# Sending the last unit of a seven-product SwiGLU by halves of tokens, and a job that runs its own last products

## The chip, the cores and the metric

One core of one Trainium2 chip. The metric is the device time of one launch in microseconds (us); lower is better. The engines are named as in the profile: PE is TensorE (PEld its weight loads), DVE is VectorE, ACT is ScalarE, POOL is GpSimd, SP is SyncE. SPq is the queue on which SP issues DMAs, POOLq that of POOL.

## The reference, cut to what matters

The kernel is one step of a hybrid streaming encoder over 1072 tokens (16 meta tokens, 1024 new frames, 32 frames of a running stream). Two feed-forward nets (FFN1 at the start, FFN2 at the end) stand around a mixing layer of attention and a recurrent branch. The change touches only the two nets:

```
def half_ffn(x, g, w_gate, w_up, w_down):
    h = rmsnorm(x, g)
    return x + 0.5 * ((jax.nn.silu(h @ w_gate) * (h @ w_up)) @ w_down)
```

The model width is 1024 and the hidden width of the nets is 2816. All operands are float32 and every product is made as three float32r products (high x high, high x low, low x high), so each operand is kept as a "hi" and a "lo" part.

## The kernel before, in words

Both nets run through the class `Seven`. It computes matrix products in a Strassen-like form, with seven block products in place of eight. The names of the operands on the token side are B11, T3, B21, T2, T4, T1, B22. The hidden width is cut into 22 chunks of 128 and these into 11 pairs, called **units** 0 to 10. The tokens are cut into four quarters of `qw` columns (268 in FFN1, 264 in FFN2): a half `b` (0 or 1) of the tokens and, in it, a token block `th`.

**The gate and up products** (`rest`, `unit`). For each unit two passes are made, gate and up, each of seven steps (`first` to `seventh`), each step for b = 0 and b = 1. A step is 12 matmuls for one b. Steps one, three and four copy their bank out on ACT; the others are added and multiplied on DVE. Only in the up pass of the last unit are all seven steps of b = 0 made ahead of those of b = 1, because then the operands of b = 0 (tiles xh0 and xl0) come free early and the next stage can load into them.

**Sending** (`send`). When a unit's result g is complete, its seven operands for the down products are formed: for four of them a subtraction on DVE (L359), for each a hi copy on ACT (L219) and a lo subtraction on DVE (L220) into a place, and then one DMA on POOL's queue (L371) into `mid_dram`. Each send covers both halves b: 128 x 2 x 264 or 268 columns, hi and lo, 536 or 528 KB. The places are `R` (one buffer) and `st` (one buffer), by turns. The works wait in the list `later`, and `tick` takes one of them after every second step (after every step in the gate pass of the last unit). The last unit's seven works are all sent from within `down`, four ahead of its first products and three behind them. They use the places of the list `stages`: R, e, e, st, s, s, R. Here "e" are two tiles that operands of the last unit leave free, and "s" two tiles of partial sums of that unit. Unit 2 is later loaded into the two "e" places and into `st`.

**The down products** (`down`). A **job** accumulates two units into two chunks of the output. It has seven products p1 to p7; p1 fills a bank `pv`, which ACT copies to a bank `pu` (L618), and p4 adds to `pu`. The results go out on ACT (first time, L612) or DVE (L609). The first four jobs take unit 0 alone, for one b at a time (3 matmuls a product, banks ps_z and ps_o). The jobs of the main run take two units and both b (12 matmuls a product). In `run` the order of the products of one job is p1, p6 of the job before, p2, p3, p7 of the job before, p4, p5: the last two products of a job are run within the next job. A job marked "end" has its p4 ahead of its p3, its p6 ahead of its p5, and its p7 at the very end. While jobs run, the order of PE's instructions is fixed by hand (`PE.on`). Elsewhere, and on the other engines throughout, the framework's scheduler puts the instructions of an engine into an order at build time by its own estimate of when each can start, the earlier in the program first; on the chip each engine runs that order.

**Loading** (`Home`, `home`). The operands of a unit are read back from `mid_dram` on SP's queue: one transfer for each b, and one or two more for the operands that do not fit. Units use three sets of places by turns (unit number modulo 3). Unit s+1 is loaded when the jobs of step s begin, into the places of unit s-2. In the main run steps s = 1 to 10 have two jobs each, (0, 1) or (2, 3); step 9 has only job 0 and step 10 only job 2. Thus unit 10 is loaded into the places of unit 7, which the second job of step 8 is the last to read, and job 2 of step 10 reads it first.

`lanes` reads and splits the weights of a job (raw, g, whi, wlo), on SP's queue, ACT and DVE.

Of the kernel before, what the change touches and what calls it, by code (L numbers as in the profile page):

```python
# [9 lines left out]
F32 = mybir.dt.float32  # L10
F32R = mybir.dt.float32r
BF16 = mybir.dt.bfloat16
AF = mybir.ActivationFunctionType
ALU = mybir.AluOpType
AX = mybir.AxisListType

P = 128
# [14 lines left out]
NAMES = ("B11", "T3", "B21", "T2", "T4", "T1", "B22")  # L32
D_FF = 2816
FC = D_FF // P
# [48 lines left out]
def tile_encoder_step(ctx, tc, x_prompt, x_sample, cache_k, cache_v, state_hgrn, meta_tokens,  # L83
# [4 lines left out]
    nc = tc.nc  # L88
# [129 lines left out]
    def split(dst_h, dst_l, src):  # L218
        A.activation(dst_h, src, AF.Copy)  # L219
        V.tensor_tensor(dst_l, src, dst_h.bitcast(F32), op=ALU.subtract)  # L220
# [108 lines left out]
    class Seven:  # L329
# [6 lines left out]
        def __init__(self, pool, t0, qw, w_gate, w_up, mids, tags, homes):  # L336
            self.pool, self.t0, self.qw, self.w_gate, self.w_up, self.tags = pool, t0, qw, w_gate, w_up, tags
            self.mids, self.homes = mids, homes
            self.B, self.X, self.ahead = {}, {}, {}
            self.gs, self.later, self.groups = [], [], 0  # L340
            self.stages = ["R", "e", "e", "st", "s", "s", "R"]

        def tile(self, name, shape, dt=F32):
            tag, bufs = self.tags[name]
# [6 lines left out]
        def send(self, i, gs):  # L351

            def part(c, th):
                return gs[c][:, self.t0:].rearrange("p (b t n) -> p b t n", b=2, t=2)[:, :, th]

            def away(name, v, left=None, right=None):
                def work():
                    if left is not None:
                        V.tensor_tensor(v, left, right, op=ALU.subtract)  # L359
                    at = self.stages.pop(0) if i == FC // 2 - 1 else ("R", "st")[len(self.later) % 2]  # L360
                    shape = [P, 2, 2, self.qw]
                    if at == "R":
                        st = base.tile(shape, F32R, tag="R", name="st")
                    elif at == "st":
                        st = self.pool.tile(shape, F32R, tag="st", name="st", bufs=1)
                    elif at == "e":
                        st = self.early.pop(0)
                    else:
                        st = self.tile(at, shape, F32R)
                    split(st[:, :, 0], st[:, :, 1], v)  # L370
                    nc.gpsimd.dma_start(self.mids[i, :, :, NAMES.index(name)], st.bitcast(F32))  # L371
                self.later.append(work)
            b11, b12, b21, b22 = (part(c, th) for c in range(2) for th in range(2))
            away("B11", b11)
            away("T1", b11, b12, b11)
            away("B21", b21)
            away("T3", b12, b22, b12)
            away("B22", b22)
            away("T2", b22, b22, b11)
            away("T4", b21, b21, b22)  # L380

        def tick(self, every=2):
            self.groups += 1
# [38 lines left out]
        def unit(self, w, i, gs, gate):  # L422

            qw, where, hilo, X = self.qw, self.where, self.hilo, self.X
            raws = []
            for x in range(2):
                raw = self.tile("raw2", [P, D]) if x else wp.tile([P, D], F32, tag="raw", name="raw", bufs=2)
                c = 2 * i + x
                nc.sync.dma_start(raw.rearrange("p (k m) -> p k m", k=KC),
                                  w[0][:, c * P:(c + 1) * P].rearrange("(k p) m -> p k m", p=P))  # L430
                raws.append(raw)
            a11, a12, a21, a22 = (r[:, x:x + 512] for r in raws for x in (0, 512))
            A11, A12 = hilo(raws[0], D)
            sa = self.tile("S", [P, D])
            s2, s1 = sa[:, :512], sa[:, 512:]
            V.tensor_tensor(s1, a21, a22, op=ALU.add)
            V.tensor_tensor(s2, s1, a11, op=ALU.subtract)
            S2, S1 = hilo(sa, D)
            sb = self.tile("S", [P, D])
            V.tensor_tensor(sb[:, :512], a11, a21, op=ALU.subtract)  # L440
            V.tensor_tensor(sb[:, 512:], a12, s2, op=ALU.subtract)
            S3, S4 = hilo(sb, D)
            A22, = hilo(a22, 512)

            def out(c, th, b, part, ps):
                to = where(gs[c], th, b)
                if gate:
                    if part is not None:
                        V.tensor_tensor(to, part, ps[:, :qw], op=ALU.add)
                    silu(to, ps[:, :qw] if part is None else to)  # L450
                else:
                    if part is not None:
                        V.tensor_tensor(part, part, ps[:, :qw], op=ALU.add)
                    V.tensor_tensor(to, ps[:, :qw] if part is None else part, to, op=ALU.mult)

            parts = [self.tile("s", [P, 4, qw]) for b in range(2)]
            x, y, z = {}, {}, {}

            def first(b):
                x[b] = bank(rotate=True)  # L460
                product(x[b], A11, X["B11", b], True)
                A.activation(parts[b][:, 0], x[b][:, :qw], AF.Copy)

            def second(b):
                z[b] = bank(rotate=True)
                product(z[b], A12, X["B21", b], True)
                out(0, 0, b, parts[b][:, 0], z[b])

            def third(b):
                product(x[b], S2, X["T2", b], False)  # L470
                A.activation(parts[b][:, 1], x[b][:, :qw], AF.Copy)

            def fourth(b):
                y[b] = bank(rotate=True)
                product(y[b], S1, X["T1", b], True)
                A.activation(parts[b][:, 2], y[b][:, :qw], AF.Copy)

            def fifth(b):
                product(x[b], S3, X["T3", b], False)
                out(1, 1, b, parts[b][:, 2], x[b])  # L480

            def sixth(b):
                product(y[b], S4, X["B22", b], False)
                out(0, 1, b, parts[b][:, 1], y[b])

            def seventh(b):
                product(x[b], A22, X["T4", b], False)
                out(1, 0, b, None, x[b])

            steps = first, second, third, fourth, fifth, sixth, seventh  # L490
            if i == FC // 2 - 1 and not gate:
                for b in range(2):
                    for step in steps:
                        step(b)
            else:
                for step in steps:
                    for b in range(2):
                        step(b)
                    self.tick(1 if i == FC // 2 - 1 else 2)

        def rest(self):
            for i in range(1, FC // 2):
                gs = [self.tile("g", [P, T]) for _ in range(2)]
                self.unit(self.w_gate, i, gs, True)
                self.unit(self.w_up, i, gs, False)
                while self.later:
                    self.later.pop(0)()
                self.send(i, gs)

        class Home:  # L510

# [62 lines left out]
        def down(self, w, resid, final, after, early):  # L574
# [70 lines left out]
            def run(jobs):  # L645

                queue, count, every = [], [0], [1]

                def step(product):
                    product()  # L650
                    count[0] += 1
                    if queue and count[0] % every[0] == 0:
                        queue.pop(0)()
                before = None
                for job in jobs:
                    step(job.p1)
                    if before:
                        step(before.p6)
                    step(job.p2)
                    step(job.p4 if job.done == "end" else job.p3)  # L660
                    if before:
                        step(before.p7)
                        if before.done:
                            queue += before.done()
                            every[0] = max(1, 20 // len(queue))
                    step(job.p3 if job.done == "end" else job.p4)
                    if job.done == "end":
                        step(job.p6)
                    step(job.p5)
                    before = job  # L670
                if before.done != "end":
                    before.p6()
                before.p7()
                while queue:
                    queue.pop(0)()

# [29 lines left out]
            def steps():  # L706
                for s in range(1, last + 1):
                    for mp in ((0, 1) if s % 2 else (2, 3)):
# [8 lines left out]
                        job = Job([(units[s - 1], W, 0), (units[s], W, 1)], mp)  # L717
                        if s == last and mp == 2:
                            job.done = "end"
                        yield job  # L720

            psum("pairs")
# [1133 lines left out]
```

## Time and profile before

| | |
|---|---|
| three runs | 2469.76, 2469.8 and 2472.51 us, median 2469.8 |
| the profiled execution | 2468.0 us, of which the span of its instructions is 2466.2 |
| busy in the span | PE 97%, PEld 93%, DVE 68%, ACT 41%, POOL 10% |
| granted TensorE clock | 0.994 of full speed over the span |
| FFN1's last up pass, b = 1, and its first down jobs | about 503 to 531 us of the span |
| end of FFN1's main run of jobs | about 683 to 722 |
| the same two places in FFN2 | about 2200 to 2226 and 2378 to 2414 |

The page's first part gives busy time by engine. The timeline lists instructions with their start and length; a bracket behind a row gives how long the engine stood idle before it and what ended that idle time. The view of windows gives busy time by stretch, with the granted clock (PEclk) and the share of the core's 16 DMA engines. The view of the DMA queues splits traffic between q1 (transfers issued by SP) and q0 (those issued by POOL), and gives for each issue the time from issue to landing.

### The profile page before, as it was taken

How to read it: one execution, taken by the hardware profiler on the slowest of the kernel's cores; microseconds unless marked ns; L12 is line 12 of the kernel's file. 1: busy time of each engine (PE TensorE's matmuls, PEld its weight loads, DVE VectorE, ACT ScalarE, POOL GpSimd, SP SyncE). 2: the span in 40 equal slices, each digit the busy share in tenths (PEclk: the TensorE clock that was granted, in tenths of full speed). 3: DMA queues.
4: the chain of work that ended last, by engine and by line, in shares of the span. 5: the costliest groups of instructions: out<-in, count | busy, mean ns of one | idle time of the engine just before them, and what ended most of it. 6: DMA issues, size and time to landing. Idle time of an engine off the chain costs nothing.

```text
span 2466.2 us, 47916 instructions
## 1 busy us (share of the span) xinstructions
PE 2396.0 (97%) x19500; PEld 2292.9 (93%) x19500; DVE 1669.0 (68%) x3144; ACT 1017.8 (41%) x2129; POOL 257.1 (10%) x461
## 2 busy tenths in 40 slices
PE   6999999999999999999999999999799999999997
PEld 5999999989999998899888888999799999999997
DVE  4866676767766477764666665556966767676876
ACT  6444444442225233332445544323444444453223
POOL 1011010100003012121000000112011111110000
PEclk9999999999999999999999999999899999999999
DMA  7334343487652111111211122522234444468761
GB/s 199 106 127 164 124 168 123 160 315 280 244 211 79 50 44 48 57 48 50 59 45 45 49 67 62 193 87 100 75 130 150 140 150 141 152 239 323 272 237 72
DMA packets 270371, 331.93 MB, mean 135 GB/s; under 512 B 41078, under 2 KB 228726, under 8 KB 264518
## 3 DMA queue, kind: packets, MB, share of 16 engines
q1 hardware_dynamic: 247942, 244.96, 29.7%
q0 software_dynamic: 22208, 83.91, 9.0%
q8 instruction: 153, 2.51, 0.4%
q14 instruction: 68, 0.56, 0.1%
HBM read 213.93 MB, written 114.89 MB: 133 GB/s over the span
## 4 chain that ended last, share of the span: by engine, by line
PE 84%; DVE 5%; issue 5%; DMA 4%; ACT 2%; POOL 1%; SPq 0%; DVEq 0%; ACTq 0%; POOLq 0%
PE ps_mm L103 28%; PE ps_z L103 26%; PE ps_o L103 9%; PE pu L103 6%; PE ps_tr L103 5%; PE pf L103 4%; PE pv L103 4%; PE ps_tr L106 2%; DMA mid_dram<-st 1%; DMA raw<-in_ffn_w_down_dram 1%; PE ps_z L106 1%; DMA u_xl<-mid_dram 1%; DVE wlo L203 1%; POOL mid_dram L371 1%; PE ps_mm L106 0%
## 5 line engine op out<-in xcount | busy, mean ns | idle before, releaser
L103 PE MATMUL ps_mm<-xh,whi 128*128 128x384 f32 (+2 forms) x960 | 320.0, 334 | 0.5 <-DVE raw L1487 0.5
L103 PE MATMUL ps_mm<-xh,wlo 128*128 128x384 f32 (+2 forms) x960 | 313.2, 326 | 0.0
L103 PE MATMUL ps_mm<-xl,whi 128*128 128x384 f32 (+2 forms) x960 | 312.8, 326 | 0.0
L219 ACT ACTIVATE whi<-S 128x1024 fp32r<-128x1024 f32 x122 | 129.3, 1059 | 311.3 <-PE ps_z L103 135.7
L371 POOL DMA_DIRECT2D mid_dram<-st x150 | 104.3, 706 | 830.4 <-DVE st L220 805.5
L103 PEld LDWEIGHTS ps_mm<-xh,whi 128*128 128x128 f32 x960 | 181.1, 189 | 9.1 <-issue 5.0
L103 PEld LDWEIGHTS ps_mm<-xl,whi 128*128 128x128 f32 x960 | 181.0, 189 | 1.2
L103 PEld LDWEIGHTS ps_mm<-xh,wlo 128*128 128x128 f32 x960 | 181.2, 189 | 0.3
L220 DVE TENSOR_TENSOR wlo<-S,whi 128x1024 fp32r<-128x1024 f32 x122 | 149.1, 1222 | 34.3 <-ACT whi L219 31.4
L220 DVE TENSOR_TENSOR st<-g,st 128x536 fp32r<-128x536 f32 (+1 forms) x150 | 104.7, 710 | 85.8 <-ACT st L219 85.8
L202 ACT ACTIVATE whi<-raw 128x1024 fp32r<-128x1024 f32 x67 | 70.4, 1056 | 180.9 <-PE ps_mm L103 139.1
L1279 DVE TENSOR_TENSOR_SCAN left<-left,oneb 128x512 f32<-128x512 f32 (+6 forms) x112 | 107.4, 959 | 54.8 <-ACT left L119 54.2
L220 DVE TENSOR_TENSOR wlo<-raw,whi 128x1024 fp32r<-128x1024 f32 x80 | 76.6, 957 | 75.4 <-ACT whi L219 73.6
L219 ACT ACTIVATE st<-g 128x536 fp32r<-128x536 f32 (+1 forms) x150 | 94.5, 643 | 79.4 <-DMA mid_dram<-st 63.8
L103 PE MATMUL ps_z<-acc1s,whi 128*128 128x268 f32 (+1 forms) x480 | 106.3, 285 | 0.0
L103 PE MATMUL ps_z<-xh1s,whi 128*128 128x268 f32 (+1 forms) x360 | 102.8, 286 | 0.0
L103 PE MATMUL ps_z<-xl1s,whi 128*128 128x268 f32 (+1 forms) x360 | 102.6, 285 | 0.0
L103 PE MATMUL ps_z<-xh1s,wlo 128*128 128x268 f32 (+1 forms) x360 | 102.6, 285 | 0.0
L103 PE MATMUL ps_z<-xh2s,whi 128*128 128x268 f32 (+1 forms) x352 | 100.4, 285 | 0.0
L103 PE MATMUL ps_z<-xl2s,whi 128*128 128x268 f32 (+1 forms) x352 | 100.3, 285 | 0.0
L103 PE MATMUL ps_z<-xh2s,wlo 128*128 128x268 f32 (+1 forms) x352 | 100.1, 285 | 0.0
L203 DVE TENSOR_TENSOR wlo<-raw,whi 128x1024 fp32r<-128x1024 f32 x67 | 82.8, 1241 | 25.1 <-ACT whi L202 21.3
(715 smaller groups left out, 7603.8 us busy)
## 6 DMA issues: line engine op xcount, KB each, us to landing
mid_dram<-st POOLq DMA_DIRECT2D x75, 536.0 KB, 3.9
mid_dram<-st POOLq DMA_DIRECT2D x75, 528.0 KB, 4.0
raw<-in_ffn_w_gate_dram SPq DMA_DIRECT2D x44, 512.0 KB, 3.7
raw<-in_ffn_w_up_dram SPq DMA_DIRECT2D x44, 512.0 KB, 3.8
raw<-in_w_in_dram SPq DMA_DIRECT2D x44, 512.0 KB, 3.7
raw<-in_ffn_w_down_dram SPq DMA_DIRECT2D x40, 512.0 KB, 6.1
u_xl<-mid_dram SPq DMA_DIRECT2D x8, 1608.0 KB, 6.6
u_xh<-mid_dram SPq DMA_DIRECT2D x8, 1608.0 KB, 10.8
```

Of the source, the lines that this page charges most:

```text
L103: return self.queue(nc.tensor.matmul(*args, **more))
L106: return self.queue(nc.tensor.transpose(*args, **more))
L202: A.activation(hi, raw, AF.Copy)
L203: V.tensor_tensor(lo, raw, hi.bitcast(F32), op=ALU.subtract)
L219: A.activation(dst_h, src, AF.Copy)
L220: V.tensor_tensor(dst_l, src, dst_h.bitcast(F32), op=ALU.subtract)
L371: nc.gpsimd.dma_start(self.mids[i, :, :, NAMES.index(name)], st.bitcast(F32))
L1279: V.tensor_tensor_scan(rev(st[:rows]), rev(st[:rows]), one, 1.0 if carry is None else carry[:rows], op0=ALU.mult, op1=ALU.mult)
```

## The change

It has two parts, and both act in FFN1 and in FFN2.

First, the last unit's sends. In the up pass of the last unit, `send` is now called between the seven steps of b = 0 and those of b = 1. It makes fourteen works in place of seven, each for one half b (one descriptor row of 264 or 268 columns, hi and lo, per partition). One of the seven works of b = 0 is taken after each step of b = 1. The seven of b = 1 are sent from within `down` as before, four ahead of its first jobs and three behind. The places are now R, st, R, st, e, e, R, and each place holds two successive half sends: R the first two, st the next two, R again two, st again the seventh of b = 0 and the first of b = 1, the two "e" the next four of b = 1, R a third time the last two. The "s" places are not used any more.

Second, in the main run the second job of step 8 is marked "tight" and is run in the order of an "end" job: p1, p6 of the job before, p2, p4, p7 of the job before, p3, p6, p5, p7. The job after it then has no products of a job before to run.

```
-            self.stages = ["R", "e", "e", "st", "s", "s", "R"]
+            self.stages, self.half = ["R", "st", "R", "st", "e", "e", "R"], []
...
-            def away(name, v, left=None, right=None):
+            def away(name, bs, v, left=None, right=None):
                 def work():
                     if left is not None:
-                        V.tensor_tensor(v, left, right, op=ALU.subtract)
...
+                        V.tensor_tensor(v[:, bs], left[:, bs], right[:, bs], op=ALU.subtract)
+                    if not final:
+                        st = place()
                     else:
...
+                        if not self.half:
+                            tile_ = place()
+                            self.half += [tile_[:, x:x + 1] for x in range(2)]
+                        st = self.half.pop(0)
+                    split(st[:, :, 0], st[:, :, 1], v[:, bs])
+                    nc.gpsimd.dma_start(self.mids[i, :, bs, NAMES.index(name)], st.bitcast(F32))
                 self.later.append(work)
...
+            for bs in (slice(0, 1), slice(1, 2)) if final else (slice(0, 2),):
+                away("B11", bs, b11)
+                away("T1", bs, b11, b12, b11)
+                away("B21", bs, b21)
+                away("T3", bs, b12, b22, b12)
+                away("B22", bs, b22)
+                away("T2", bs, b22, b22, b11)
+                away("T4", bs, b21, b21, b22)
...
             if i == FC // 2 - 1 and not gate:
-                for b in range(2):
-                    for step in steps:
-                        step(b)
+                for step in steps:
+                    step(0)
+                self.send(i, gs)
+                for step in steps:
+                    step(1)
+                    self.later.pop(0)()
...
+                    tight = job.done in ("end", "tight")
                     if before:
                         step(before.p6)
                     step(job.p2)
-                    step(job.p4 if job.done == "end" else job.p3)
+                    step(job.p4 if tight else job.p3)
...
-                    step(job.p3 if job.done == "end" else job.p4)
-                    if job.done == "end":
+                    step(job.p3 if tight else job.p4)
+                    if tight:
                         step(job.p6)
                     step(job.p5)
                     before = job
+                    if tight:
+                        step(job.p7)
+                        before = None
...
+                        if s == last - 2 and mp == 3:
+                            job.done = "tight"
```

## Rows read from the trace of the kernel before

**Rows 1.** The page's first part: busy us, share of the span, instructions.
```profile
PE 2396.0 (97%) x19500; PEld 2292.9 (93%) x19500; DVE 1669.0 (68%) x3144; ACT 1017.8 (41%) x2129; POOL 257.1 (10%) x461
```

**Rows 2.** Windows: stretch, length, busy by engine, clock, DMA share, GB/s.
```profile
503.00:514.00 11.00, 10.96 (x87) 10.64 (x87) 6.92 (x16) 4.86 (x8) 0.69 (x1) 1.00 0.96 387
514.00:519.00 5.00, 3.28 (x23) 2.63 (x21) 5.00 (x9) 3.42 (x9) 1.51 (x3) 1.00 1.03 430
519.00:523.00 4.00, 4.00 (x20) 4.00 (x21) 2.94 (x6) 2.31 (x6) 1.28 (x2) 0.57 0.99 415
523.00:531.10 8.10, 6.48 (x45) 5.57 (x43) 5.73 (x12) 6.06 (x16) 1.41 (x2) 1.00 1.01 404
...
2210.60:2216.20 5.60, 3.09 (x24) 2.66 (x22) 5.60 (x10) 3.73 (x9) 2.07 (x4) 1.00 1.04 438
2216.20:2226.30 10.10, 9.26 (x64) 8.03 (x64) 7.96 (x17) 7.87 (x21) 2.13 (x4) 1.00 1.00 404
```

**Rows 3.** Timeline of PE: start, us, operation, idle before and its releaser.
```profile
517.38 0.52 PE L103 MATMUL ps_z<-u_xh,whi 128*128 128x268 f32 x2 [0.73 <-ACT acc1s L612]
518.91 0.64 PE L103 MATMUL ps_o<-u_xh,whi 128*128 128x268 f32 x2 [0.90 <-DVE acc1s L609]
...
708.15 0.64 PE L103 MATMUL pv<-u_xl,g 128*128 128x268 f32 x3 [1.67 <-DMA u_xl<-mid_dram]
...
2216.16 0.51 PE L103 MATMUL ps_o<-u_xh,whi 128*128 128x264 f32 x2 [2.41 <-DVE acc1s L609]
...
2239.36 0.64 PE L103 MATMUL pv<-u_xh,g 128*128 128x264 f32 x3 [1.09 <-ACT pu L618]
...
2400.98 0.64 PE L103 MATMUL pv<-u_xl,g 128*128 128x264 f32 x3 [0.64 <-DMA u_xl<-mid_dram]
```

**Rows 4.** Timeline of ACT around FFN1's last unit and FFN2's first jobs.
```profile
506.45 0.65 ACT L219 ACTIVATE st<-g 128x536 fp32r<-128x536 f32 x1 [1.15 <-DVE g L454]
508.02 0.40 ACT L471 ACTIVATE s<-ps_z 128x268 f32<-128x268 f32 x1 [0.93 <-PE ps_z L103]
...
514.46 0.38 ACT L618 ACTIVATE ps_z<-ps_z 128x268 f32<-128x268 f32 x1 [0.31 <-PE ps_z L103]
...
2237.78 1.03 ACT L219 ACTIVATE g<-raw 128x256 fp32r<-128x256 f32 x3 [4.64 <-DMA raw<-in_ffn_w_down_dram]
2238.72 0.59 ACT L618 ACTIVATE pu<-pv 128x528 f32<-128x528 f32 x1
```

**Rows 5.** Timeline of DVE around FFN1's last unit.
```profile
502.24 0.44 DVE L454 TENSOR_TENSOR g<-s,g 128x268 f32<-128x268 f32 x1
...
507.92 0.43 DVE L454 TENSOR_TENSOR g<-ps_o,g 128x268 f32<-128x268 f32 x1
...
515.22 0.70 DVE L359 TENSOR_TENSOR g<-g 128x536 f32<-128x536 f32 x1
```

**Rows 6.** DMA queues from 508.3 to 518.7: packets, MB, share of 16 engines.
```profile
q1 hardware_dynamic: 320, 3.70, 88.4%
q0 software_dynamic: 144, 0.55, 12.9%
```

**Rows 7.** DMA queues from 522 to 528.
```profile
q0 software_dynamic: 209, 0.83, 33.5%
```

**Rows 8.** The send issued at 508.30 by itself, then that at 437.41: us to landing.
```profile
mid_dram<-st POOLq DMA_DIRECT2D x1, 536.0 KB, 10.4
...
mid_dram<-st POOLq DMA_DIRECT2D x1, 536.0 KB, 5.4
```

**Rows 9.** ACT in steady state: a row of the timeline, and the view of waits.
```profile
442.94 0.65 ACT L219 ACTIVATE st<-g 128x536 fp32r<-128x536 f32 x1 [3.10 <-DMA mid_dram<-st]
...
ACT st L219 <- DMA mid_dram<-st: 63.8, 53, 4.4
```

**Rows 10.** SP's queue, loading unit 10 in FFN1; the chain, two products of one job.
```profile
696.84 1.07 SPq L519 DMA_DIRECT2D u_xl<-mid_dram  x2
...
690.50 2.98 PE pu L103 x24
```

More of the change, by code (lines that the diff above doesn't have):

```diff
@@ L354, in part, with place @@
                 return gs[c][:, self.t0:].rearrange("p (b t n) -> p b t n", b=2, t=2)[:, :, th]
-            def away(name, v, left=None, right=None):
+            final = i == FC // 2 - 1
+            def place():
+                at = self.stages.pop(0) if final else ("R", "st")[len(self.later) % 2]
+                shape = [P, 2, 2, self.qw]
+                if at == "R":
+                    return base.tile(shape, F32R, tag="R", name="st")
+                if at == "st":
+                    return self.pool.tile(shape, F32R, tag="st", name="st", bufs=1)
+                return self.early.pop(0) if at == "e" else self.tile(at, shape, F32R)
@@ L357, in work @@
+            def away(name, bs, v, left=None, right=None):
                 def work():
                     if left is not None:
-                        V.tensor_tensor(v, left, right, op=ALU.subtract)
[L360 to L367, printed above, removed]
-                    else:
-                        st = self.tile(at, shape, F32R)
@@ L370, in work @@
-                    split(st[:, :, 0], st[:, :, 1], v)
-                    nc.gpsimd.dma_start(self.mids[i, :, :, NAMES.index(name)], st.bitcast(F32))
+                        V.tensor_tensor(v[:, bs], left[:, bs], right[:, bs], op=ALU.subtract)
+                    if not final:
+                        st = place()
+                    else:
+                        if not self.half:
+                            tile_ = place()
+                            self.half += [tile_[:, x:x + 1] for x in range(2)]
+                        st = self.half.pop(0)
@@ L372, in away @@
+                    split(st[:, :, 0], st[:, :, 1], v[:, bs])
+                    nc.gpsimd.dma_start(self.mids[i, :, bs, NAMES.index(name)], st.bitcast(F32))
                 self.later.append(work)
             b11, b12, b21, b22 = (part(c, th) for c in range(2) for th in range(2))
[L374 to L380, printed above, removed]
+            for bs in (slice(0, 1), slice(1, 2)) if final else (slice(0, 2),):
[6 more added lines that the diff above has]
+                away("T4", bs, b21, b21, b22)
@@ L505, in rest @@
                 self.unit(self.w_up, i, gs, False)
-                while self.later:
+                while self.later and i < FC // 2 - 1:
                     self.later.pop(0)()
-                self.send(i, gs)
+                if i < FC // 2 - 1:
+                    self.send(i, gs)
         class Home:
@@ L659, in run @@
                     step(job.p2)
-                    step(job.p4 if job.done == "end" else job.p3)
+                    step(job.p4 if tight else job.p3)
                     if before:
                         step(before.p7)
-                        if before.done:
+                        if callable(before.done):
                             queue += before.done()
                             every[0] = max(1, 20 // len(queue))
-                    step(job.p3 if job.done == "end" else job.p4)
-                    if job.done == "end":
+                    step(job.p3 if tight else job.p4)
+                    if tight:
                         step(job.p6)
@@ L670, in run @@
                     before = job
-                if before.done != "end":
+                    if tight:
+                        step(job.p7)
+                        before = None
+                if before:
                     before.p6()
-                before.p7()
+                    before.p7()
                 while queue:
```

## The prediction

> **What bounds the kernel now.** I read the page's first part: PE is busy 97% of the span [rows 1], so a change of order can only win what PE loses. Next I read the windows around the places that the change touches. In FFN1 PE is full up to 514, then loses 1.7 of 5.0 us, runs 4.0 us at a granted clock of 0.57 (most of that at 1.2 GHz, the lower of its two levels, after PE's idle time), and loses 1.6 of 8.1 [rows 2]. In FFN2 it loses 2.5 of 5.6 and 0.8 of 10.1. DVE and ACT show why: from 514 to 519 DVE is busy all 5.00 us and ACT 3.42. These are the first small jobs (3 matmuls a product), and the last unit's sends run among them. The timeline of PE names single waits: 0.73 and 0.90 us for ACT and DVE in FFN1, 2.41 for DVE in FFN2, and 1.09 in FFN2 for a copy on ACT [rows 3]. At the end of the main run PE waits 1.67 and 0.64 us for the load of unit 10 [rows 3]. So at most some 12 us are to be had in all.
>
> **Part 1, the work that is halved and moved.** A whole operation of a send takes 0.65 us on ACT [rows 4] and 0.70 on DVE [rows 5]; one of 268 columns takes 0.39 and 0.43 by the nearest rows [rows 4, 5]. The seven half sends of b = 0 are 7 x 0.39 = 2.7 us of ACT and (7 + 4) x 0.43 = 4.7 us of DVE. One whole send stands in that stretch already, so the net additions are 2.1 and 4.0 us. From 503 to 514 ACT has 6.1 us free and DVE 4.1 [rows 2]. It just fits on DVE: I count 0, and up to 1 us for each net if it does not. POOL issues 14 DMAs in place of 7 and is nearly idle (10%) [rows 1]: 0.
>
> What leaves the small jobs is 4 subtractions and 6 lo parts, 10 x 0.27 = 2.7 us of DVE, and 6 x 0.26 = 1.6 us of ACT. Of PE's listed waits there I let 1.6 us go in FFN1 (0.73 + 0.90) and 1.7 of the 2.41 in FFN2. The ends are 0 and, in FFN1, 3.1 (with the 1.5 us that 20 matmuls lost at the low clock: they took 4.0 us, at the pace of the windows around them 2.5).
>
> **Part 1, the waits that are added.** The sends of b = 0 have only R and st, two halves in each, and use each place twice within some 10 us. The second use has to wait until both DMAs of the first have landed. The wait falls on ACT, which makes the hi copy first, and everything behind it on ACT waits too. That this happens is in the trace: in steady state ACT stood 53 times, 63.8 us in all, for `mid_dram<-st`; at 442.94 it had stood 3.10 us [rows 9]. That send was issued at 437.41 and took 5.4 us to land [rows 8], so ACT had come to the copy 442.94 - 3.10 - 437.41 = 2.4 us after the issue. The build's order reckons with such a landing, and the chip's is longer. In steady state PE has slack for it. It has none where a copy that PE needs stands behind: at 2237.78 ACT had stood 4.64 us for a DMA, the copy to pu came late at 2238.72 [rows 4], and that is PE's 1.09 us at 2239.36 [rows 3].
>
> How late do the landings come? From about 502 SP's queue holds the loads of units 0 and 1, and POOL's queue gets little: 0.55 MB from 508.3 to 518.7, a share of 12.9% against 88.4% [rows 6], or 53 KB/us; the one send issued at 508.30 took 10.4 us [rows 8]. From 522 it is 0.83 MB in 6 us, 138 KB/us [rows 7]. A half send is 0.27 MB, about 5.2 us at the first pace.
>
> The operands of b = 0 are complete at 502.24 + 0.44 = 502.7, except b21, which is at 507.92 + 0.43 = 508.4 [rows 5]. Of the sends, B11 can go before the crowd. T1 is issued at about 504.4 (0.43 + 0.39 + 0.43 and hand-overs behind 502.7) and lands at about 510. B22 takes R again: ACT reaches its copy at about 504.4 + 2.4 = 507 and stands till 510, with the copy that stood at 508.02 [rows 4] behind it. T4 takes st again, which holds B21 and T3. In POOL's queue B21 is third or fourth behind T1 and T3. Three halves are 0.82 MB: 505 + 0.82 / 0.053 = 520.5. Four are 1.10 MB: 0.90 by 522, and 0.20 / 0.138 = 1.4 more, 523.4. I take 522. By the build's reckoning B21 would land near 512, so T4's copy is put ahead of the first job's copy from pv, which stood at 514.46 [rows 4]; B11 of b = 1, in the same place, is put ahead of it too. That copy now comes at 522 + 2 x 0.39 + 0.1 = 522.9, 8.4 us late (6.9 to 9.8), and p4 of the first job, and with PE's fixed order all behind it, waits. The earlier wait is inside this one. The third use of R waits for the fifth half, 1.37 MB, at 525.4; T2 of b = 1 is by then not yet due. Less the 1.7 us that shorter sends save, FFN1 pays 6.7 us. FFN2 has the same order and the same crowd (DMA share 1.00 and above [rows 2]): 8.4 - 1.5 = 6.9, and its 1.09 us at 2239.36 goes, because PE comes later than the weights: 5.8 us.
>
> Here a rule speaks against my price. The Trainium skill, DMA: Bandwidth & Descriptors, section Anatomy of one DMA, gives a fit for DMAs issued from GpSimd, 2.0 us plus the bytes at 436 GB/s. An estimate by it is 2.6 us for a half send, and by that the places would be free in time. The 10.4 us of the one send [rows 8], where the fit gives 3.3, disagree in this stretch; the rival "in time" below is what would hold by it.
>
> SP's queue: the loads of unit 2 into the "e" places still stand ahead of weights of the main run, and wait for later sends. But the DMA engines are full, the bytes are the same, and PE is later, so I count 0. The loads of units 0 and 1 give POOL 12.9% some 3 us earlier, 0.4 us, also under the wait.
>
> **Part 2.** Two products of a job take 2.98 us on PE [rows 10], one 1.49. The xl places of unit 7 were free after nine products from the start of that job (its own first five, two of the job before, p1 of the next and its own p6); now after eight. The next reader of unit 10 has fourteen products ahead of it both before and after. So the load, issued at 696.84 [rows 10], starts 1.49 us earlier: 1.67 falls to 0.18, and 0.64 to 0. Gain 2.1 us. If the load takes longer by as much, 0. In the tight job p6 and p7 write the same bank with only p5 between, 1.49 us for DVE to read 536 columns (0.70 for an operation of that size [rows 5]); up to 0.5 us is lost if a weight split stands before it. What is late next there is nothing that PE waits for in the rows.
>
> **The sum.** +6.7 + 5.8 - 2.1 = +10.4 us on the profiled execution's 2468.0 (span 2466.2): 2478.4. The median of the runs stands 1.8 higher: 2480.
>
> **The rivals.** *In time:* the places come free before ACT gets to them. Then only gains are left: 1.6 in FFN1, 1.7 + 1.1 in FFN2, 2.1 at the ends of the main runs, 6.5 in all, 2463. For it: with 138 KB/us [rows 7] from the start three halves need 6 us and land by 511. Against it: that pace came only when SP's queue was thinning out, and here its loads are at their thickest. It is the case on the other side, and it decides by whether B21 lands before about 513. *Partly covered:* ACT's built order puts the small jobs' copies ahead of T4, or the order of the queue lets B21 go first; the waits then cost 1 to 4 us a net and the gains offset them, 2466 to 2474, about 2470. *Worse:* B21 fourth, less saved, and the clock falls during the longer stop as at 519 [rows 2], 1.5 us a net, and no gain in part 2: 2486. I count it with the forecast.
>
> **How the numbers follow.** The forecast with its worse end, 0.55; partly covered, 0.20; in time, 0.25. A measurement of this kernel can tell about 0.2% (4.9 us) from no change. So slower 0.55, same 0.20, faster 0.25. The forecast's own range is 2475 to 2486; the range with the others is 2463 to 2486.
>
> **What would show it.** Right: in FFN1 an idle row of ACT of over 5 us before a copy into st, released by DMA `mid_dram<-st`, and PE idle some 6 to 9 us in the first small jobs, released by ACT; the same in FFN2; half sends that land 5 to 15 us after issue. Part 2 right: the load of unit 10 issued about 1.5 us earlier against the job's start, and PE's wait for it under 0.3 us. Wrong: ACT's idle rows there under 1 us, or PE's 2.41 us gone with nothing in its place.

## The result, and the profile after

The changed kernel takes 2483.9 us (median of four runs, 2482.6 to 2484.7) against 2469.8 before (four runs, 2467.5 to 2472.5): a ratio of 1.006, 95% interval 1.0049 to 1.0072. It is slower, by 14 us. The profiled execution took 2484.7, its span 2482.9; the spans of the two traces differ by 16.7 us. The lines of the code have moved: the subtraction is L370, the send L379, the steps' copies L480 and L485, the jobs' outputs L622 and L625, the copy after p1 L631.

The first part of the page after, to set beside [rows 1]: PE's busy time grows by 3.5 us only, so 13 us of the 16.7 are idle time.

```profile
PE 2399.5 (97%) x19500; PEld 2298.5 (93%) x19500; DVE 1671.4 (67%) x3166; ACT 1018.2 (41%) x2143; POOL 261.6 (11%) x475
```

The windows after, over the stretches of FFN1 in [rows 2] and over FFN2's (stretch, length, busy us by engine, clock, DMA share, GB/s):

```profile
503.00:514.00 11.00, 7.98 (x63) 7.56 (x61) 5.10 (x12) 1.66 (x4) 1.08 (x2) 0.96 0.99 370
514.00:519.00 5.00, 4.02 (x18) 4.02 (x19) 4.01 (x9) 2.71 (x6) 1.61 (x3) 0.50 1.02 432
519.00:523.00 4.00, 3.71 (x26) 3.49 (x25) 0.94 (x3) 0.00 (x0) 0.00 (x0) 0.87 1.02 405
523.00:531.10 8.10, 2.78 (x12) 2.78 (x13) 4.29 (x10) 4.01 (x10) 2.13 (x4) 0.74 0.97 404
...
2212.00:2217.00 5.00, 1.99 (x17) 1.78 (x15) 0.00 (x0) 0.00 (x0) 0.00 (x0) 0.95 0.98 393
2217.00:2232.00 15.00, 8.13 (x46) 7.92 (x47) 7.31 (x17) 5.54 (x13) 2.69 (x5) 0.73 1.01 418
```

There are stretches in which whole engines stand still: from 519 to 523 ACT does nothing, from 2212 to 2217 neither ACT nor DVE. The DMA engines are full all the while (share 1.02 and 0.98). The timeline of ACT names the reason (start, us, operation, idle before and its releaser):

```profile
506.19 0.63 ACT L219 ACTIVATE whi<-raw 128x512 fp32r<-128x512 f32 x1 [0.41 <-PE ps_mm L103]
514.22 0.43 ACT L219 ACTIVATE st<-g 128x268 fp32r<-128x268 f32 x1 [7.40 <-DMA mid_dram<-st]
514.55 0.38 ACT L480 ACTIVATE s<-ps_z 128x268 f32<-128x268 f32 x1
...
525.98 0.74 ACT L219 ACTIVATE st<-g 128x268 fp32r<-128x268 f32 x2 [8.48 <-DMA mid_dram<-st]
...
527.89 0.37 ACT L631 ACTIVATE ps_z<-ps_z 128x268 f32<-128x268 f32 x1
...
2218.28 0.42 ACT L219 ACTIVATE st<-g 128x264 fp32r<-128x264 f32 x1 [8.37 <-DMA mid_dram<-st]
...
2229.15 0.74 ACT L219 ACTIVATE st<-g 128x264 fp32r<-128x264 f32 x2 [7.62 <-DMA mid_dram<-st]
```

ACT stops twice in each net, each time before the hi copy of a half send into a place whose last send is still under way (the places R and st both bear the name `st` in the rows). Right behind the first stop stands a step's copy (514.55), behind the second the first job's copy after p1 (527.89). Those are what PE waits for:

```profile
514.98 0.59 PE L103 MATMUL ps_z<-acc1s,whi 128*128 128x268 f32 x1 [4.00 <-ACT s L480]
...
528.32 1.04 PE L103 MATMUL ps_z<-u_xh,g 128*128 128x268 f32 x3 [5.61 <-ACT ps_z L631]
...
717.91 0.64 PE L103 MATMUL pv<-u_xl,g 128*128 128x268 f32 x3 [0.38 <-DMA u_xl<-mid_dram]
...
2219.03 0.81 PE L103 MATMUL ps_z<-acc2s,whi 128*128 128x264 f32 x2 [5.04 <-ACT s L480]
...
2231.16 1.03 PE L103 MATMUL ps_z<-u_xh,g 128*128 128x264 f32 x3 [4.84 <-ACT ps_z L631]
```

Four waits of PE, 19.5 us together, where [rows 3] had 0.73, 0.90 and 2.41. (The three matmuls at 528.32 take 1.04 us; three of that size take 0.64 at 717.91: PE comes back at the lower clock, granted 0.50 from 528 to 530.) The 1.67 at the end of FFN1's main run is 0.38, the 0.64 in FFN2 and the 1.09 [rows 3] are not there any more. ACT's view of waits (us in all, times, longest) against 63.8, 53 and 4.4 [rows 9]:

```profile
ACT st L219 <- DMA mid_dram<-st: 101.0, 59, 8.5
```

The transfers: the queues from 506 to 517, and the sends issued at 505.96, 516.69 and 533.15, each by itself (size, us to landing).

```profile
q1 hardware_dynamic: 329, 3.82, 86.6%
q0 software_dynamic: 160, 0.55, 12.4%
...
mid_dram<-st POOLq DMA_DIRECT2D x1, 268.0 KB, 8.2
...
mid_dram<-st POOLq DMA_DIRECT2D x1, 268.0 KB, 9.2
...
mid_dram<-st POOLq DMA_DIRECT2D x1, 268.0 KB, 2.3
```

A half send takes 8 to 10 us while SP's queue is full of loads (the five issued between 505 and 518 took 8.2 to 10.3) and 2.3 when that queue has run out.

Both kernels issue 19500 matmuls, in the same order except within the tight job of each net (96 matmuls a net), so their starts can be set side by side, matmul by matmul. This table is worked out from the two traces in that way:

| matmul | before | after | after less before |
|---|---|---|---|
| FFN1, last before the first stop | 509.18 | 510.70 | 1.5 |
| last before the second stop | 514.51 | 522.42 | 7.9 |
| soon after the second stop | 516.37 | 530.94 | 14.6 |
| in the main run | 552.53 | 563.63 | 11.1 |
| after the load of unit 10 | 708.15 | 717.91 | 9.8 |
| FFN2, last before the first stop | 2205.96 | 2213.71 | 7.8 |
| last before the second stop | 2211.24 | 2226.03 | 14.8 |
| soon after the second stop | 2213.08 | 2233.74 | 20.7 |
| in the main run | 2248.61 | 2266.21 | 17.6 |
| after the load of unit 10 | 2400.98 | 2417.82 | 16.8 |

So the stretch of the two stops, up to the main run, costs FFN1 9.6 us and FFN2 9.8 (this is what "the first jobs cost" means below); the ends of the main runs give back 1.3 and 0.8. The first 1.5 and the 2.0 that go between the nets lie in work that the change does not touch.

### The profile page after: what moved, and what is told of

Read it like the earlier page. It is cut to its first block, busy times and chain, and to the rows that moved or that the text cites. A ratio compares the mean times of both kernels' runs of the same rounds, so it can differ in the third digit from the quotient of the medians.

```text
span 2482.9 us, 47977 instructions
## 1 busy us (share of the span) xinstructions
PE 2399.5 (97%) x19500; PEld 2298.5 (93%) x19500; DVE 1671.4 (67%) x3166; ACT 1018.2 (41%) x2143; POOL 261.6 (11%) x475
## 4 chain that ended last, share of the span: by engine, by line
PE 55%; issue 29%; DVE 6%; POOL 4%; DMA 3%; ACT 2%; POOLq 0%; SPq 0%; DVEq 0%; ACTq 0%
PE ps_mm L103 20%; PE ps_z L103 12%; PE pu L103 6%; PE ps_o L103 5%; PE pf L103 4%; PE pv L103 4%; POOL mid_dram L379 4%; PE ps_tr L103 2%; DMA mid_dram<-st 2%; PE ps_tr L106 2%; PE ps_z L106 1%; DVE wlo L203 1%; PE ps_mm L106 0%; ACT whi L202 0%; DMA u_xl<-mid_dram 0%
## 5 line engine op out<-in xcount | busy, mean ns | idle before, releaser
L379 POOL DMA_DIRECT2D mid_dram<-st x168 | 112.0, 674 | 872.1 <-DVE st L220 845.3
L220 DVE TENSOR_TENSOR st<-g,st 128x536 fp32r<-128x536 f32 (+3 forms) x168 | 109.4, 663 | 114.3 <-ACT st L219 113.9
L219 ACT ACTIVATE st<-g 128x536 fp32r<-128x536 f32 (+3 forms) x168 | 99.6, 606 | 123.7 <-DMA mid_dram<-st 101.0
```

Source lines behind the costliest of these rows:

```text
L379: nc.gpsimd.dma_start(self.mids[i, :, bs, NAMES.index(name)], st.bitcast(F32))
```

## The experiments

Theory: the price is ACT's waits for places whose sends are slow to land, and nothing else. Rivals: the halves themselves cost (twice the sends, more operations), or the new order of the job does. Each ratio below is to the kernel before in the same set of runs (its median was 2469.5, 2466.9 and 2469.2 us in the three sets), with its 95% interval in brackets; where sets differ, the ratio is what can be compared.

### Which part

**Part 2 alone**, put into the kernel before:

```
-                    step(job.p4 if job.done == "end" else job.p3)
+                    step(job.p4 if tight else job.p3)
...
+                        if s == last - 2 and mp == 3:
+                            job.done = "tight"
```

> The kernel before with only the second part of the change: the second job of step 8 runs its own last two products. My theory: the whole loss of the change comes from its sends, and this part gains what PE's wait for the load of unit 10 loses, 1.3 us in FFN1 (1.67 to 0.38 in the profile after) and 0.6 in FFN2: 2468 us, 1.5 to 2 us under the kernel before. Rival: the new order of products loses as much elsewhere, within 0.5 us of before or above it.

Measured: 2465.4 us, ratio 0.9983 (0.9974 to 0.9992), a larger gain than expected. **Part 1 alone**, the changed kernel with the job's order of before:

> The kernel after without the second part of the change. My theory: 1.5 to 2 us above the kernel after, 2485 to 2486 us, with ACT standing 7 to 8.5 us twice in FFN1 for the DMAs out of its places, as after. Rival (the tight job is part of the loss): below the kernel after.

Measured: 2488.6, ratio 1.0072 (1.0059 to 1.0084), some 3 us over the time expected, and the two stops of FFN1 are there (7.36 and 8.35 us). Part 1 is the loss, all of it; part 2 is a small gain. In the trace of part 2 alone, PE's wait for unit 10 is what it is with both parts:

```profile
706.22 0.64 PE L103 MATMUL pv<-u_xl,g 128*128 128x268 f32 x3 [0.41 <-DMA u_xl<-mid_dram]
```

By the matmul-by-matmul difference it gains 1.3 us there and 0.7 in FFN2; the rest of the 4 us of its median is not at places that it touches, and the lower end of the interval allows 2.

### Halves, and how many go early

**No half early**: halves and tight as in the changed kernel, but all fourteen halves go from `down`.

```
-            self.stages, self.half = ["R", "st", "R", "st", "e", "e", "R"], []
+            self.stages, self.half = ["R", "e", "e", "st", "s", "s", "R"], []
...
                     step(1)
-                    self.later.pop(0)()
...
-            sends(4)
+            sends(len(self.later) - 3)
```

> The seven pairs of b=0 are sent in halves as in the changed kernel, but none inside the loop of b=1: all fourteen halves go from the down products on, as the seven whole sends did before; the half step's early p1 (tight) is kept. Theory (the cost comes from the early sends' reuse of places R and st while the transfers are slow): neither stop of ScalarE is there, the time is that of tight alone or a little under, 2462 to 2467. Rival (halving costs by itself, through twice the sends on GpSimd's queue and twice the subtractions): 2470 or more.

Measured: 2462.1, ratio 0.9981 (0.9972 to 0.9989), as expected and the same as part 2 alone (0.9983). ("None" is the order of the program: the build, which puts what is ready where an engine has room, still lets four halves go by 512, but with no copy waiting for a place.) Fourteen sends on POOL in place of seven cost nothing that can be measured. The rival falls.

**Four early**, places R, st, e, e, s, s, R, the other ten halves from `down`:

> The kernel after, but only the first four half sends of b = 0 go during the steps of b = 1 (into R and st, once each), the other ten from within the down products, into e, e, s, s, R. No place is used twice before it has long been emptied. My theory: as with its own places, no long wait on ACT; the small jobs carry three more half sends, so 1 to 2 us above the run with own places: 2465 to 2471 us. Rival 1 (halves cost by themselves): 2478 or more.

Measured: 2464.4, ratio 0.998 (0.9971 to 0.9989), just under the range; ACT has no wait of over 1 us for `mid_dram` around the last unit of either net. **Six early**, with the places so that a copy comes late after the send that it waits for:

```
+            self.stages, self.half = ["R", "st", "s", "e", "e", "R", "s"], []
...
+                    if n < 6:
+                        self.later.pop(0)()
```

> Six half sends early instead of seven, on the places R, st, s, e, e, R, s, so that no copy writes a place whose send was issued less than some 10 us before. Theory (the price is the reuse alone): both stops of ScalarE gone or under 2 us together in each net; what stays is a wait of TensorE for the first unit's upper operand of some 2 us a net, as with four early; 2465 to 2469. Rival (each early half costs by itself): 2474 or more.

Measured: 2468.2, ratio 1.0004 (0.9995 to 1.0014), inside the time expected. Neither of the two long stops is left in FFN1. In FFN2 a shorter one is, longer than the 2 us that were allowed, since the place was still not free in time, and PE waits as long behind it:

```profile
2218.40 0.42 ACT L219 ACTIVATE s<-g 128x264 fp32r<-128x264 f32 x1 [2.91 <-DMA mid_dram<-s]
...
2219.43 0.51 PE L103 MATMUL ps_z<-u_xh,whi 128*128 128x264 f32 x2 [2.91 <-ACT acc2s L626]
```

So four halves early cost nothing that can be measured where no place is used again soon, and they also gain nothing: none, four and part 2 alone cannot be told apart. Six stand 0.24% over four, outside both intervals. Matmul by matmul the first jobs of FFN2, where the short stop is, cost 2.9 us with six early and gain 1.8 with four; in FFN1, which has no stop, those with six early gain 2.2. So the stop costs, not the number of early halves. In the traces this makes some 2 us of the 6 between the two kernels; where the rest lies is not shown.

### One stop instead of two

```
-            self.stages, self.half = ["R", "st", "R", "st", "e", "e", "R"], []
+            self.stages, self.half = ["R", "st", "s", "s", "e", "e", "R"], []
```

> The kernel after with one change: the list of places is R, st, s, s, e, e, R, so that no send of b = 0 and none of the first of b = 1 uses a place again (the first "s" tile is free once the steps of b = 0 are made, the second after the sixth step of b = 1). Halves, early sends and the tight job stay. My theory: the loss is ACT's wait for a place to be emptied. ACT's idle time for mid_dram there falls under 1 us each, PE's 4.0 and 5.6 us in FFN1 and 5.0 and 4.8 in FFN2 go, and the time is 2464 to 2469 us. Rival 1 (halves cost by themselves: more operations on a full DVE): 2478 or more. Rival 2 (the early sends crowd the loads of units 0 and 1): PE waits for u_xh at the first job instead, 2 to 3 us a net, about 2470 to 2474.

Measured: 2479.5, ratio 1.0037 (1.0025 to 1.005). The expectation missed, for a reason that the trace points to: the second "s" seems to have been given the buffer of the first, so the second stop stayed, on "s" in place of "st". The last send out of the first "s", issued at 507.50, took 12.6 us, to 520.1, and the copy into the second starts right then.

```profile
520.18 0.74 ACT L219 ACTIVATE s<-g 128x268 fp32r<-128x268 f32 x2 [9.96 <-DMA mid_dram<-s]
...
515.47 0.64 PE L103 MATMUL ps_z<-u_xh,g 128*128 128x268 f32 x3 [1.97 <-DMA u_xh<-mid_dram]
...
522.52 1.04 PE L103 MATMUL ps_z<-u_xh,g 128*128 128x268 f32 x3 [6.04 <-ACT ps_z L631]
```

What it does show: the first stop is gone from ACT's timeline, and the kernel is 0.23% nearer to before (1.006 against 1.0037, some 5.7 us). With one stop the first jobs cost FFN1 5.7 us and FFN2 6.9 (matmul by matmul, to the main run), against 9.6 and 9.8 with both. And in these stands a wait that the first stop had covered, 1.97 us in FFN1 for unit 0's load.

### Why the halves land late

**Shorter rows on SP's queue.** The loads of units 0 to 2 go as one transfer for each operand, so a partition's row is 2144 bytes in place of the whole record.

```
+                if self.i < 3:
+                    for x in range(n):
+                        nc.sync.dma_start(t[:, x].bitcast(F32), ff.mids[self.i, :, b, x])
```

> The changed kernel, but the loads of the first three units on SP's queue are issued as one transfer for each operand, so that a partition's row is 2144 bytes instead of the whole 12.8 KB record. Theory A (the share of GpSimd's sends in the crowded stretch hangs on the size of the rows that stand against them): a half send lands in 3 to 5 us instead of 8 to 10, ScalarE's two waits shrink under 3 us each, and the time is 2468 to 2477. Theory B (the share is one of bytes outstanding or of queues, not of rows): landings stay at 8 to 10 us and the time at 2482 to 2486.

Measured: 2475.1, ratio 1.0028 (1.0017 to 1.0039). The queues from 506 to 517, and the two stops:

```profile
q1 hardware_dynamic: 1670, 3.18, 82.0%
q0 software_dynamic: 224, 0.78, 17.5%
...
512.01 0.43 ACT L219 ACTIVATE st<-g 128x268 fp32r<-128x268 f32 x1 [6.31 <-DMA mid_dram<-st]
...
520.49 0.74 ACT L219 ACTIVATE st<-g 128x268 fp32r<-128x268 f32 x2 [5.21 <-DMA mid_dram<-st]
```

The time is in theory A's range, but its landings are not: the five halves issued from 504 to 515 took 5.2 to 7.8 us, where 3 to 5 were expected, and POOL's share rose from 12.4% to 17.5% only. But the share over 11 us hides two phases. The sends issued at 505.96 and 506.55 in the changed kernel moved no packet until 509.81; in this run those issued at 504.82 and 505.42 moved none until 509.29. While their packets moved, the queues were, in the changed kernel from 509.8 to 516.5 and in this run from 509.2 to 512.5:

```profile
q1 hardware_dynamic: 194, 2.21, 78.9%
q0 software_dynamic: 160, 0.55, 20.4%
...
q1 hardware_dynamic: 387, 0.74, 58.6%
q0 software_dynamic: 160, 0.55, 41.4%
```

So with the short rows POOL's share doubled once its packets moved, and the 3.9 to 4.5 us before the first packet stayed. What holds the sends back there is not shown. SP also had less outstanding here (its 24 transfers of 0.27 MB went out one by one from 502.09 to 521.73; the changed kernel's four of 1.6 MB had all been issued by 511), so the size of the rows and the amount ahead are not told apart by this run.

**Less outstanding, rows as they are.** All seven early halves on the changed kernel's places; unit 1's two loads stand behind both of unit 0's and wait there until the last early half is written (`ff.gate` is that half's place).

```
+                if self.i == 1:
+                    nc.gpsimd.tensor_copy(t[:, 0, 0, 0:1], ff.gate[:, 0, 0, 0:1])
                 nc.sync.dma_start(t.bitcast(F32), ff.mids[self.i, :, b, 0:n])
```

> The changed kernel with all seven early halves on its own places; the two loads of unit 1 (1.6 MB each, their operands first used near 530 to 543) are held on SP's queue until the last early half is written, by an element that GpSimd copies into the place. The rows and sizes of the transfers stay as they are. Theory (the early halves are slow because SP's loads of both units are outstanding at the same time, so the reuse of their places stalls ScalarE): with unit 0's loads alone against them the halves land in 4 to 6 us instead of 8 to 10, the two stops of ScalarE shrink from 7.4 and 8.5 us to under 3 us each, and the time is 2464 to 2474. Rival (the halves land in 8 us whatever stands against them, or unit 1 comes late instead): 2479 or more.

Measured: 2475.1, ratio 1.0022 (1.0013 to 1.0032), 1 us above the range. ACT's stops, the queues and the halves' landing from 512.4 to 518.6, and then the halves issued from 503 to 512:

```profile
511.25 0.43 ACT L219 ACTIVATE st<-g 128x268 fp32r<-128x268 f32 x1 [6.42 <-DMA mid_dram<-st]
...
518.00 0.74 ACT L219 ACTIVATE st<-g 128x268 fp32r<-128x268 f32 x2 [3.48 <-DMA mid_dram<-st]
...
q1 hardware_dynamic: 102, 1.11, 41.8%
q0 software_dynamic: 241, 0.82, 32.9%
mid_dram<-st POOLq DMA_DIRECT2D x3, 268.0 KB, 4.3
...
mid_dram<-st POOLq DMA_DIRECT2D x2, 268.0 KB, 7.8
```

Half of the theory holds. Once unit 0's load has thinned out, the halves land in 4.3 us and the second stop shrinks from 8.48 to 3.48. The halves before it stood against unit 0's loads and one of 0.55 MB for the residual, and still took 7.8, so the first stop hardly moved (7.40 to 6.42). Half of SP's loads are enough to make them slow. The cost falls to 4.0 us in FFN1 and 4.6 in FFN2.

### What comes next on the path

Without the stops PE waited for unit 0's load, 1.47 and 1.45 us with no half early. Two kernels put that load first: with four early and units 0 and 1 in each other's places,

```
-                tag, n = ((("xh0", 6), ("xh1", 6)), (("xl0", 6), ("xl1", 6)), (("xh2", 4), ("xl2", 4)))[j][b]
+                tag, n = ((("xl0", 6), ("xl1", 6)), (("xh0", 6), ("xh1", 6)), (("xh2", 4), ("xl2", 4)))[j][b]
```

> Four early halves on places that are free (as in e5_four_early), and units 0 and 1 change homes, so that unit 0's load is issued ahead of the other on SP's queue. In e5_four_early TensorE waited some 2 us a net for unit 0's upper operand. If that wait hangs on the order of issue: it goes, and the time is 2460 to 2463. If the load lands late whatever its turn, because the loads together fill the engines: 2464 to 2466, unchanged.

and with none early and unit 1's loads held as above, until the half of B21 is written:

> The kernel with halves, tight, and none sent early (e4_none_early), and unit 1's loads held until the half of B21 is written, so that unit 0's loads have the engines first. There TensorE waited 1.47 and 1.45 us for unit 0's upper operand. If that wait is the next thing on the path: it goes, and the time is 2458 to 2461. Rival (the stretch from 503 to 543 is bound by the transfers together, near 400 GB/s, and what is gained at its start is lost at its end, where ScalarE waits for the weights): 2461 to 2464, unchanged.

Measured: 2462.8, ratio 0.9984 (0.9975 to 0.9992), and 2465.0, ratio 0.9983 (0.9974 to 0.9992). By its time the first is in the range where the wait goes and time is won, and the second is over both ranges, but the kernel before differed as much between the two sets. By the ratios both are unchanged beside 0.998 and 0.9981, although the wait is gone or small in both (0.40 and 0.70 us in the first, none in the second). In FFN1 what was won at 515 is lost at 542. The first kernel's ACT and PE, then the second's:

```profile
540.95 0.42 ACT L219 ACTIVATE g<-raw 128x256 fp32r<-128x256 f32 x1 [6.04 <-DMA raw<-in_ffn_w_down_dram]
...
541.92 0.64 PE L103 MATMUL pv<-u_xl,g 128*128 128x268 f32 x3 [1.79 <-ACT pu L632]
...
541.79 1.03 ACT L219 ACTIVATE g<-raw 128x256 fp32r<-128x256 f32 x3 [3.85 <-DMA raw<-in_ffn_w_down_dram]
...
543.90 0.82 PE L103 MATMUL pu<-u_xe,whi 128*128 128x268 f32 x2 [2.14 <-DVE acc0s L625]
```

ACT waits for the next weights, which stand at the end of a stretch that the transfers fill: the DMA share is 0.99 of the 40 us from 503 to 543 in the first of these kernels, at 396 GB/s; before, 1.01 at 402. That would also explain why early sends gain nothing: in the changed kernel only the first half goes ahead of SP's four loads of 1.6 MB (499.78, landed in 5.5 us; the loads are issued from 503.22), the second is issued at 505.96, when the engines are full. That from there on the order only settles which transfer goes first is argued, not shown.

No kernel beats part 2 alone. It, none early, four early and the two last lie between 0.998 and 0.9984, each with an interval of about 0.001 to either side.

## Why the prediction was right, and which terms were mis-sized

Forecast 2480, slower, own range 2475 to 2486; measured 2483.9. The mechanism was the one named: reuse of R and st, ACT in order, PE's copies behind it, the same in both nets. The sum was 3.9 us short of the median and 6.3 short of the profiled execution. That the time still lies in the range is in part luck: the upper end was made of other items (B21 fourth, the clock, no gain in part 2) than the one that failed. Two of the signs named were not met as they stood: PE's wait in the first small jobs was 5.61 and 4.84 us, not 6 to 9, because the rest stood in the up pass (4.00 and 5.04), and the wait for unit 10 in FFN1 was 0.38, not under 0.3.

- **The size of the added wait** (8.4 us, FFN1 +6.7, FFN2 +5.8) is the step that failed: +9.6 and +9.8. "The earlier wait is inside this one" was wrong. The copy that waited for T1 stopped ACT until 514.22, and B21's own hi copy stood behind it, so B21 was issued at 516.69 (T1 and T3 had gone at 505.96 and 506.55), and landed at 525.88 in place of 522. A stop that delays the sends which the next stop waits for adds to it. With one stop alone the first jobs cost 5.7 and 6.9 us, where 6.7 and 5.8 were worked out for one; these costs also hold PE's waits for unit 0's load (1.97 and 2.37 us), so they are no clean test of the price.
- **T1's landing** (about 510) was 514.15; it was issued where it was forecast (505.96, of which 1.5 is this execution's lateness, against 504.4). I took 5.2 us for a half, at 53 KB/us [rows 6]. All five in the crowd took 8.2 to 10.3, and of T1's 8.2 the first 3.9 passed before a packet of it moved. Two halves in the queue at once share the same 53 KB/us; that pace was right (0.55 MB from 506 to 517, 50 KB/us), the number of sends in it was not.
- **Copies behind the wait**: the first job's copy was forecast at 522.9, and came at 527.89, 1.5 of which this execution was late already. What I had not seen is that in the up pass too a copy stands behind the stop (514.55) and PE waits for it, 4.00 us. I had named that copy, [rows 4] at 508.02, and given it no price of its own.
- **The clock**: counted with "worse", 1.5 us a net. It fell in the forecast case too: 0.50 from 514 to 519 and 0.74 from 523 to 531.1. Between 514.98 and the second stop PE loses 2.2 us more, and in the first jobs 1.2.
- **What leaves the small jobs** (1.6 and 1.7 us): after the second stop PE regains 3.1 us in FFN1 by 541 (14.6 to 11.5), the upper end that was named, and 2.2 in FFN2 at the place of the wait of 2.41 (20.7 to 18.5), of which 0.7 is lost again by 2235 (19.2). The sum took off 1.7 in FFN1 and 1.5 in FFN2, where the working before it had 1.6 and 1.7; that is 0.1 us in all.
- **What was counted as 0**: DVE's and POOL's added work. Right, by the runs with none and with four early. A half's hi copy took 0.43 us, where 0.39 was taken.
- **Part 2** (2.1 us): right. Unit 10's load is issued at 706.43, with PE 11.1 us late by then; at 696.84 + 11.1 = 707.9 it would have been as before, so 1.5 us earlier, as reckoned. The gains are 1.3 and 0.8, and the wait 0.38 where 0.18 was forecast.
- **The rival "in time"**: it would have needed B21 landed before 513, and T1, the second half of all, came at 514.15. The estimate of 2.6 us by the fit of the Trainium skill (DMA: Bandwidth & Descriptors, Anatomy of one DMA) is about what a half takes when SP's queue moves nothing, 2.3 us at 533.15; beside a load on SP's queue 8 to 10 was measured. Something like "partly covered" is what six early halves show, in another kernel: one short stop, of 2.91 us, and no change from before.

## What to carry to other kernels

Before a transfer is moved earlier, look at whether the DMA engines have room at the new time: here they were full from 503 to 543 (share 1.01 before the change), and a send that was moved into that stretch became a long one. The place that it leaves from is then held for the long time, and an engine that works in order and waits for the place also holds back every copy behind it; count the reuse by the landing times of that stretch, and count stops one after the other, since the first also delays the sends on which the second waits. Where PE waits for the last of a set of places, letting a job finish its own reads first is a small gain (2.0 us here, at the two places where it was wanted).

## What was not expected of the hardware

A 268 KB send on POOL's queue took 2.3 us when SP's queue had run out, 4.3 when SP's queue had 41.8% of the engines, and 8 to 10 when it had 86.6%. Much of this is time before the first packet. The send issued at 437.41 in the kernel before moved its first packet after 1.7 us, the two issued at 505.96 and 506.55 after the change not before 509.81, while SP's queue alone filled the engines from 506 to 509.8:

```profile
q1 hardware_dynamic: 118, 1.39, 98.1%
```

Over the whole of 506 to 517 POOL's queue moved 160 packets of the profile to 329 of SP's (3.4 and 11.6 KB each). But from 509.8 to 516.5, when its packets moved, it was 160 to 194, not far from one for one, and 144 to 164 for the send of 508.30 in the kernel before (512.4 to 518.4). With the short rows it was 160 to 387 (3.4 and 1.9 KB), and POOL's share of the engines 41.4% in place of 20.4%. The Trainium skill (DMA: Bandwidth & Descriptors, Queues, rings and completion order) says that an engine turns from one queue to the next after a packet of some 9 to 17 descriptors; what a packet of that sense holds here no run shows, and the counts with the short rows are not one for one. Whether the shorter rows or the smaller amount ahead of it raised POOL's share stays open, and so does what holds a send back before its first packet.
